# Deciding the top-k selection partly on GpSimd, cutting its ends into small steps, and splitting a third of the key blocks on GpSimd

## The chip, the cores and the metric

One NeuronCore of a Trainium2 chip runs the whole layer as one program. The metric is the device time of an execution in microseconds (us); the median of several executions counts. Engines: TensorE (PE), VectorE (DVE), ScalarE (ACT), GpSimd (POOL), and SyncE (SP), whose queue issues nearly all DMAs.

## What is computed

One layer of a streaming encoder on 2048 tokens of 1024 channels: a sparse attention with a learned index, a pooling mixer, gates, two layer norms and a gated feed-forward with a short convolution. What the change touches is the index and the attention:

```python
rel = relu(einsum('bqhd,bsd->bqhs', q_idx, k_idx) * idx_scale)        # 8 index heads
idx_score = einsum('bqh,bqhs->bqs', w_idx * head_w_scale, rel)        # one score per query and key
idx_score = where(admissible, idx_score, -inf)                        # chunk-causal
_, sel = top_k(idx_score, 256)                                        # each query keeps 256 keys
s = einsum('bqhd,bqkd->bqhk', q, k_lat[sel]) * attn_scale             # 8 heads, latent 128
p = softmax(where(valid, s, -inf)); out = einsum('bqhk,bqkd->bqhd', p, v_lat[sel])
```

## The kernel before

Matrix products in float32 are made of three passes: each operand is split into a rounded high part and a remainder, and `mm3` multiplies high by high, high by low and low by high. A split is two instructions (`split`, L394): normally a copy on ACT and a subtraction on DVE; with `pool=True` both on POOL.

The tokens are 16 blocks of 128, in 4 groups. The program runs the index projection of all groups, then for each group the pooling, query and gate projections (`run`, L2043), then attention (`attention`, L1377), the mixing and output projection, and the feed-forward. It is written out as one long list of instructions per engine, so each engine's order is fixed when the program is built.

**The selection as background work.** The reference's top-k and gather are replaced by a mask per block, added to the scores of all keys. `select` (L1069) finds each query's 256th largest index score by bisection on the bits of the float, 32 rounds. In each round every block's scores are counted against the trial value, part on DVE (`is_ge` with an accumulated sum), part on ACT (`Sign` with an accumulated sum). The blocks form two halves; `decide` (L1090) then makes the next trial value `F` of one half while the other half is counted: three small DVE instructions `g`, `h`, `F` on at most 4 columns. After the last round come the **ends**, block by block: a count of the strictly larger scores, a `Sign` on ACT, then on DVE a comparison, a running sum over the whole row (`tensor_tensor_scan`, L1162), two more comparisons and a subtraction, and the mask, which SP stores. There are three selections (`GROUPS`, L65): groups 0 and 1 together, group 2, group 3 (blocks 12 to 15).

These steps are generators. `turn` (L430), called after each small piece of the main work, decides at build time how many background steps go in: a credit grows by `RATE` (0.75) times the modelled PE time and each step costs its modelled DVE or ACT time; no step goes in while the modelled backlog of DVE or ACT behind PE is `SLACK` (3 us) or more. One `yield` of `select` ends a step.

**Attention.** A unit is one group of queries and one head, 32 in all, group after group. `scores` (L1229) makes scores and softmax weights of one block row after another; `values` (L1280) goes over the key blocks: four PE transposes into PSUM, a split of the result (ACT copy from PSUM, DVE subtraction from PSUM), and `LAG` = 3 key blocks later the product with the values. Once per unit POOL splits the next unit's queries (`split_q`, L1224). `load_mask` (L1192) fetches the mask of a block one block ahead of its use. If its selection has not ended, it runs the background work to the end on the spot:

```python
            while self.selected < b:
                if next(self.bg[0][1], "end") == "end":
                    self.bg.pop(0)
            self.settle()
            nc.sync.dma_start(m, self.d_msk[b])
```

All compute instructions are issued by one helper, so nearly all rows of the profile have its line, L133; tile names tell them apart: `m,cd<-b,F` a count on DVE, `g`, `h`, `F` the decision, `b<-p,b` the subtraction of a split from PSUM, `b<-m` and `b<-m,b` on POOL the split of the queries, `mx` (CUSTOM_DVE_ANT_0) the masked scores with their row minimum, `msk` a mask in memory, `vv` values, `q` queries.

## Time and profile before

| | |
|---|---|
| median of 3 runs (lowest, highest) | 3157.49 us (3157.08, 3163.70) |
| the profiled execution, its span | 3163.64 us, 3161.9 us |
| PE busy, mean granted clock | 3041.3 us (96%), 0.987 |
| DVE, ACT, POOL busy | 2433.5 (77%), 1605.4 (51%), 540.3 us (17%) |
| PE waits in the stretch 1308 to 1394 us: for DVE, three kinds | 24.3, 4.2, 2.7 us |

Times of instructions are in us from the span's start. Busy shares over the whole span mix stages with different limits; the rows further down are of single stretches. A busy PE is not always a PE at its peak, so the number of matmuls in a stretch is read beside its busy time.

### The profile page before, as it was taken

The numbers are of one execution on the slowest core, as the hardware profiler recorded it, in microseconds if no ns is written. First come the engines' busy times: TensorE is split into PE (matmuls) and PEld (weight loads), VectorE is DVE, ScalarE is ACT, GpSimd is POOL, SyncE is SP. The second block draws the span as 40 slices with busy tenths as digits, with TensorE's granted clock in tenths as the row PEclk, the third lists the DMA queues.
The fourth block names the chain that finished last, engine by engine and source line by source line (L and its number), as shares of the span: only waits on it lengthen the run. The fifth ranks groups of instructions, "written<-read, shape, count | busy, mean of one in ns | idle before, by whom it ended". The sixth has DMA issues, their size and how long they took to land. (4 is left out here: it accounts for less than half of the span.)

```text
span 3161.9 us, 43884 instructions
## 1 busy us (share of the span) xinstructions
PE 3041.3 (96%) x14750; PEld 2536.5 (80%) x14750; DVE 2433.5 (77%) x4552; ACT 1605.4 (51%) x3073; POOL 540.3 (17%) x528
## 2 busy tenths in 40 slices
PE   8999999999999999879999999999999999999998
PEld 8887778888888787768787778887778888888887
DVE  4578877896789899988775588998886655667776
ACT  3468846773578788657611144444442222433253
POOL 2002010010010221110231234554411111100011
PEclk9999999999999999989999999999999999999999
DMA  6758783765366332222264778887888866998753
GB/s 247 246 202 295 272 311 141 284 222 214 136 245 252 111 95 77 71 78 70 81 226 158 258 259 303 295 298 281 291 310 315 316 213 224 365 399 327 266 196 110
DMA packets 325872, 715.88 MB, mean 226 GB/s; under 512 B 27466, under 2 KB 132366, under 8 KB 325646
## 3 DMA queue, kind: packets, MB, share of 16 engines
q1 hardware_dynamic: 317006, 697.34, 62.0%
q10 hardware_dynamic: 8640, 15.73, 1.3%
q8 instruction: 117, 1.92, 0.3%
q14 instruction: 109, 0.89, 0.1%
HBM read 454.85 MB, written 258.11 MB: 225 GB/s over the span
## 5 line engine op out<-in xcount | busy, mean ns | idle before, releaser
L133 PE MATMUL p<-b,b 128*128 128x512 f32 (+3 forms) x12568 | 2828.8, 381 | 83.2 <-DVE mx L133 30.7
L133 PEld LDWEIGHTS p<-b,b 128*128 128x128 f32 x12568 | 2258.5, 190 | 524.6 <-DVE b L133 36.9
L133 DVE TENSOR_TENSOR b<-p,b 128x512 fp32r<-128x512 f32 (+3 forms) x626 | 395.4, 658 | 151.8 <-PE p L133 99.7
L133 ACT ACTIVATE b<-p 128x512 fp32r<-128x512 f32 (+11 forms) x638 | 363.2, 606 | 278.9 <-PE p L133 265.9
L133 ACT ACTIVATE b<-b 128x512 fp32r<-128x512 f32 (+3 forms) x344 | 270.8, 805 | 322.5 <-DVE b L133 138.5
L133 DVE TENSOR_TENSOR b<-b,b 128x1024 fp32r<-128x1024 f32 (+6 forms) x302 | 338.9, 1133 | 84.3 <-ACT b L133 37.1
L133 ACT ACTIVATE m<-b,F 128x448 bf16<-128x448 f32 (+3 forms) x448 | 366.1, 820 | 47.9 <-DVE F L133 34.3
L133 DVE TENSOR_SCALAR_CACHE_REDUCE m<-b,F 128x512 bf16<-128x512 f32 (+6 forms) x476 | 372.5, 808 | 8.3 <-DMA gm<-m 4.3
L133 ACT ACTIVATE b<-m 128x512 fp32r<-128x512 f32 x215 | 133.2, 627 | 332.4 <-DVE m L133 119.9
L133 DVE SCALAR_TENSOR_TENSOR b<-b,cw,b 128x1023 f32<-128x1023 f32 (+1 forms) x176 | 246.3, 1411 | 69.7 <-ACT b L133 68.7
L133 ACT ACTIVATE b<-b,cw 128x1024 f32<-128x1024 f32 x88 | 106.9, 1236 | 270.8 <-DVE b L133 270.8
L133 POOL TENSOR_TENSOR b<-b,b 128x1024 f32<-128x1024 f32 (+3 forms) x62 | 148.6, 2401 | 491.0 <-DVE b L133 283.2
L133 PE MATMUL p<-ident,b 128*128 128x128 f32 x1248 | 198.1, 278 | 17.4 <-DVE b L133 7.0
L133 ACT ACTIVATE b<-b,mx 128x1024 f32<-128x1024 f32 (+2 forms) x192 | 171.5, 895 | 81.0 <-DVE mx L133 79.0
L133 DVE TENSOR_TENSOR b<-m,b 128x512 fp32r<-128x512 f32 x215 | 153.8, 723 | 55.0 <-ACT b L133 52.9
L133 PEld LDWEIGHTS p<-ident,b 128*128 128x128 f32 x1248 | 154.0, 142 | 52.5 <-DVE b L133 11.4
L133 DVE SCALAR_TENSOR_TENSOR b<-b,ws,b 128x768 f32<-128x768 f32 (+5 forms) x154 | 153.4, 1023 | 55.5 <-ACT b L133 53.0
L133 DVE CUSTOM_DVE_ANT_0 b<-p,b 128x1024 f32<-128x1024 f32 (+7 forms) x128 | 125.6, 984 | 35.0 <-PE p L133 27.2
L133 PE MATMUL p<-kst,b 128*128 128x384 f32 (+3 forms) x656 | 149.0, 360 | 2.8 <-ACT b L133 2.0
L133 ACT ACTIVATE m<-p 128x512 f32<-128x512 f32 (+2 forms) x172 | 100.7, 585 | 79.1 <-PE p L133 75.6
L133 PEld LDWEIGHTS p<-kst,b 128*128 128x128 f32 x656 | 111.7, 189 | 24.1 <-ACT b L133 13.6
L133 DVE TENSOR_TENSOR b<-p,m 128x512 f32<-128x512 f32 x132 | 89.8, 682 | 10.7 <-PE p L133 10.6
(125 smaller groups left out, 1496.7 us busy)
## 6 DMA issues: line engine op xcount, KB each, us to landing
b<-wk SPq DMA_DIRECT2D x339, 512.0 KB
wk<-b SPq DMA_DIRECT2D x211, 512.0 KB
b<-h SPq DMA_DIRECT2D x88, 512.0 KB
b<-in_w_ffn_up_dram SPq DMA_DIRECT2D x44, 512.0 KB
h<-b SPq DMA_DIRECT2D x44, 512.0 KB
b<-vv SPq DMA_DIRECT2D x80, 256.0 KB
hs<-b SPq DMA_DIRECT2D x33, 512.0 KB
b<-hs SPq DMA_DIRECT2D x33, 512.0 KB
```

What stands on the lines that cost most here:

```text
L133: return f(*args, **kw)
```

## The change

- `decide`: `g` and `h` are made by three POOL instructions, issued together behind the first count of the other half; only `F` stays on DVE.
- `RATE` 0.80 instead of 0.75; the model's cost of the running sum is doubled (`SCAN`); while a selection's end runs, a background step may go in up to a backlog of 4 us.
- The ends yield after nearly every instruction, and the running sum is cut into pieces of 512 columns, each started from the last column of the one before.
- `load_mask` also fetches the block after next, if its selection has ended.
- While background work is left and from group 1 on, every third key block's split in `values` goes another way: ACT copies PSUM to a tile, POOL makes both parts from it.

```diff
-SLACK = 3.0
+SLACK, END_SLACK = 3.0, 4.0
+PIECE = 512
-RATE = 0.75
+RATE = 0.8
-SCAN = 1.04
+SCAN = 2.12
...
-        while self.bg and self.clocks.backlog() < SLACK and self.credit > 0:
+        while self.bg and self.clocks.backlog() < (END_SLACK if self.ending else SLACK) and self.credit > 0:
...
             step = next(gen, "end")
+            self.ending = step == END
...
-            nc.vector.scalar_tensor_tensor(g_, cd, 2.0, ca, op0=OP.mult, op1=OP.subtract)
+            nc.gpsimd.tensor_scalar(g_, cd, 2.0, -lim, op0=OP.mult, op1=OP.add)
+            nc.gpsimd.tensor_tensor(g_, g_, ca, op=OP.subtract)
+            nc.gpsimd.tensor_scalar(h, g_, 0.0, float(2 ** bit) if bit < 31 else -1.0, op0=OP.is_lt, op1=OP.mult)
             yield
...
-                nc.vector.tensor_scalar(h, g_, lim, float(2 ** bit), op0=OP.is_lt, op1=OP.mult)
-                yield
                 nc.vector.scalar_tensor_tensor(f2, h, 2 ** (bit - 1) if bit else 0, F[k],
...
-                    if pend:
+                    if pend and i == 0:
                         next(pend, None)
...
-                nc.vector.tensor_tensor_scan(cu, eq, eq, 0.0, op0=OP.add, op1=OP.max)
+                yield END
+                for c0 in range(0, N, PIECE):
+                    e = slice(c0, min(c0 + PIECE, N))
+                    nc.vector.tensor_tensor_scan(cu[:, e], eq[:, e], eq[:, e], cu[:, c0 - 1:c0] if c0 else 0.0,
+                                                 op0=OP.add, op1=OP.max)
+                    yield END
...
-        if b >= NB or b in self.masks:
+        if b >= NB or b in self.masks or not wait and b > self.selected:
             return
...
                 self.load_mask(b + 1)
+            if h == 0 and rb < RB - 2 or h == H - 1 and rb >= RB - 2:
+                self.load_mask(b + 2, False)
...
-            self.split(pt[:, 0, c:], pt[:, 1, c:], ps.rearrange("p h q -> p (h q)")[:, c:])
+            src = ps.rearrange("p h q -> p (h q)")[:, c:]
+            if self.bg and g and kb % 3 == 1:
+                whole = self.T([P, 512])[:, c:]
+                nc.scalar.activation(whole, src, AF.Copy)
+                self.split(pt[:, 0, c:], pt[:, 1, c:], whole, pool=True)
+            else:
+                self.split(pt[:, 0, c:], pt[:, 1, c:], src)
```

As built, DVE issues 47 subtractions and 384 decision instructions fewer and 24 pieces of running sums more. POOL issues 576 decision instructions and 47 pairs of split instructions more. PE's 14750 matmuls are the same; from the one that ran at 1394 us on they stand in the same order.

**SP's queue where attention passes to group 3** (`vv` values, `q` queries, `msk_175` to `msk_178` the masks of blocks 12 to 15; L461 is `settle`). Before:

```order
574 L1213 DMA m_15969<-q_158 128x1x512
575 L461 DMA at_181<-m_15906 128x512
576 L461 DMA msk_175<-b_15913 128x1664
577 L1206 DMA b_15910<-msk_175 128x1664
582 L461 DMA msk_176<-b_15991 128x1792
583 L1206 DMA b_15978<-msk_176 128x1792
585 L461 DMA msk_177<-b_16077 128x1920
586 L1206 DMA b_16040<-msk_177 128x1920
587 L461 DMA msk_178<-b_16151 128x2048
588 L1206 DMA b_16138<-msk_178 128x2048
```

Now (L440 is `turn`):

```order
564 L440 DMA msk_177<-b_15615 128x1920
568 L1221 DMA m_15911<-q_157 128x1x512
569 L440 DMA at_181<-m_15852 128x512
573 L1221 DMA m_16133<-q_158 128x1x512
574 L440 DMA msk_178<-b_16098 128x2048
578 L1214 DMA b_16235<-msk_175 128x1664
579 L1214 DMA b_16296<-msk_176 128x1792
580 L1221 DMA m_16350<-q_158 128x1x512
586 L1214 DMA b_16359<-msk_177 128x1920
587 L1214 DMA b_16406<-msk_178 128x2048
```

Before, each of the four masks was stored by `settle` right ahead of its load. Now all four are stored by `turn` before the first is loaded (the stores of blocks 12 and 13 are rows 531 and 548).

**DVE at the running sum of block 14** (`SCALAR_TENSOR_TENSOR` with one input is a running sum; `p` is PSUM). Before:

```order
2315 L133 TENSOR_TENSOR b_16035<-p_4869_16033,b_16035 128x128
2316 L133 TENSOR_SCALAR b_16066<-b_16065 128x1920
2317 L133 SCALAR_TENSOR_TENSOR b_16067<-b_16066 128x1920
2318 L133 TENSOR_TENSOR m_16132<-p_4827_15872,m_16133 64x512
2319 L133 SCALAR_TENSOR_TENSOR nd_16072<-b_16067,fx_16051,cg_16050 128x1
2321 L133 TENSOR_SCALAR b_16066<-b_16067,nd_16072 128x1920
2322 L133 TENSOR_TENSOR b_16065<-b_16065,b_16066 128x1920
2323 L133 TENSOR_SCALAR b_16077<-b_16065 128x1920
```

Now:

```order
1746 L135 TENSOR_SCALAR b_15166<-b_15165 128x1920
1747 L135 TENSOR_TENSOR b_15196<-p_4622_15191,b_15196 128x512
1748 L135 ISA b_15217,mx_15180<-p_4627_15213,b_14619,mx_15180 128x512
1750 L135 SCALAR_TENSOR_TENSOR b_15167<-b_15166 128x512
1751 L135 TENSOR_TENSOR b_15227<-p_4629_15222,b_15227 128x512
1752 L135 SCALAR_TENSOR_TENSOR b_15167<-b_15166,b_15167 128x512
1753 L135 ISA b_15251,mx_15243<-p_4637_15244,b_14495 128x1024
1761 L135 SCALAR_TENSOR_TENSOR b_15167<-b_15166,b_15167 128x512
1764 L135 SCALAR_TENSOR_TENSOR b_15167<-b_15166,b_15167 128x384
```

The end that stood as one run of long instructions now stands as pieces between attention's own instructions.

**POOL across one unit of group 1.** Before (`b<-m` the queries' split, COPY part of a head's result):

```order
163 L133 TENSOR_SCALAR b_13977<-m_13896 128x512
164 L133 TENSOR_TENSOR b_13977<-m_13896,b_13977 128x512
165 L133 COPY m_14013<-rinv_13756 128x4x64
166 L133 COPY m_14013<-rinv_13894 128x4x64
167 L133 TENSOR_SCALAR b_14118<-m_14051 128x512
```

Now (`b<-b` a key block's split):

```order
790 L135 TENSOR_TENSOR b_14690<-b_14691,b_14690 128x512
791 L135 COPY m_14717<-rinv_14427 128x4x64
793 L135 TENSOR_SCALAR b_14755<-b_14756 128x512
794 L135 TENSOR_TENSOR b_14755<-b_14756,b_14755 128x512
795 L135 TENSOR_SCALAR b_14811<-b_14812 128x128
797 L135 TENSOR_SCALAR b_14845<-b_14846 128x512
798 L135 TENSOR_SCALAR b_14873<-m_14765 128x512
799 L135 TENSOR_TENSOR b_14845<-b_14846,b_14845 128x512
800 L135 TENSOR_TENSOR b_14873<-m_14765,b_14873 128x512
```

Three or four key blocks' splits have come into each unit, and in row 798 the queries' split stands between the two instructions of one of them.

## Rows read from the trace of the kernel before

**Rows 1.** The page: the span, PE's and DVE's line (busy us, share, instructions) and PE's line of the 40 slices (tenths).

```profile
span 3161.9 us, 43884 instructions
...
PE 3041.3 (96%) x14750; PEld 2536.5 (80%) x14750; DVE 2433.5 (77%) x4552; ACT 1605.4 (51%) x3073; POOL 540.3 (17%) x528
...
PE   8999999999999999879999999999999999999998
```

**Rows 2.** Busy time by stretch: from and to in us, length, then busy us (instructions) of PE, PEld, DVE, ACT and POOL, granted PE clock, DMA share, GB/s.

```profile
300.00:420.00 120.00, 109.50 (x479) 87.42 (x478) 105.54 (x408) 105.81 (x289) 0.10 (x1) 0.97 0.83 293
480.00:1040.00 560.00, 560.00 (x2565) 465.43 (x2564) 467.80 (x1066) 383.18 (x686) 35.86 (x50) 1.00 0.57 208
880.00:1040.00 160.00, 160.00 (x712) 132.54 (x711) 147.09 (x369) 126.03 (x229) 16.30 (x22) 1.00 0.60 224
1114.00:1308.00 194.00, 188.02 (x1122) 158.04 (x1121) 182.95 (x409) 158.94 (x336) 29.92 (x40) 1.00 0.26 78
1308.00:1394.00 86.00, 54.86 (x258) 44.59 (x258) 71.61 (x120) 39.62 (x75) 14.43 (x8) 0.80 0.26 90
1394.00:1560.00 166.00, 164.28 (x979) 139.42 (x977) 134.23 (x246) 120.74 (x233) 18.94 (x22) 1.00 0.21 66
```

**Rows 3.** What PE waited for from 1308 to 1394 us: us in total, times, longest us.

```profile
PE p L133 <- DVE mx L133: 24.3, 4, 7.9
PE p L133 <- DVE m L133: 4.2, 1, 4.2
PE p L133 <- DVE b L133: 2.7, 1, 2.7
```

**Rows 4.** The timeline around 1356 us: start, us, engine, instruction, and in brackets the idle time before and what ended it.

```profile
1355.93 4.45 DVE L133 TENSOR_TENSOR_SCAN b<-b 128x1920 f16<-128x1920 f16 x1
...
1356.46 4.98 POOL L133 TENSOR_TENSOR b<-m,b 128x512 fp32r<-128x512 f32 x1
...
1361.01 1.11 PE L133 MATMUL p<-ident,b 128*128 128x128 f32 x4 [4.20 <-DVE m L133]
```

**Rows 5.** DVE's instructions by shape from 1308 to 1394 us: count | busy us, mean ns of one | idle before.

```profile
L133 DVE TENSOR_TENSOR_SCAN b<-b 128x2048 f16<-128x2048 f16 x1 | 4.4, 4426 | 0.0
...
L133 DVE TENSOR_TENSOR_SCAN b<-b 128x1664 f16<-128x1664 f16 x1 | 3.6, 3624 | 0.0
...
L133 DVE TENSOR_TENSOR b<-p,b 128x128 fp32r<-128x128 f32 x3 | 0.8, 282 | 0.0
```

**Rows 6.** DVE's instructions by shape over the whole span, same columns.

```profile
L133 DVE SCALAR_TENSOR_TENSOR g<-cd,ca 128x2 f32<-128x2 f32 x160 | 28.5, 178 | 7.8 <-ACT m L133 3.7 <-DVE m L133 0.5
L133 DVE TENSOR_SCALAR h<-g 128x2 int32<-128x2 f32 x160 | 28.1, 176 | 4.5
...
L133 DVE TENSOR_TENSOR_SCAN b<-b 128x512 f16<-128x512 f16 x1 | 1.2, 1233 | 0.0
```

**Rows 7.** DVE's instructions by shape from 1114 to 1394 us: the splits from PSUM, the counts (in the decisions and at the ends together), and the decision's last instruction. Columns as in Rows 5.

```profile
L133 DVE TENSOR_TENSOR b<-p,b 128x512 fp32r<-128x512 f32 x110 | 72.4, 685 | 9.2 <-ACT b L133 8.6
...
L133 DVE TENSOR_SCALAR_CACHE_REDUCE m<-b,F 128x896 bf16<-128x896 f32 x12 | 13.6, 1137 | 0.0
...
L133 DVE TENSOR_SCALAR_CACHE_REDUCE m<-b,F 128x1024 bf16<-128x1024 f32 x8 | 10.0, 1273 | 0.0
...
L133 DVE TENSOR_TENSOR b<-p,b 128x256 fp32r<-128x256 f32 x16 | 6.6, 412 | 0.0
...
L133 DVE TENSOR_SCALAR_CACHE_REDUCE m<-b,F 128x768 bf16<-128x768 f32 x5 | 5.0, 1006 | 0.0
...
L133 DVE SCALAR_TENSOR_TENSOR F<-h,F 128x2 int32<-128x2 int32 x9 | 1.6, 175 | 0.2
```

**Rows 8.** POOL's splits of the queries from 1114 to 1308 us, by shape, columns as in Rows 5.

```profile
L133 POOL TENSOR_TENSOR b<-m,b 128x512 fp32r<-128x512 f32 x13 | 16.8, 1292 | 1.1
L133 POOL TENSOR_SCALAR b<-m 128x512 fp32r<-128x512 f32 x13 | 8.1, 620 | 149.0 <-PE p L133 67.3 <-ACT b L133 32.3 <-DMA m<-q 27.1
```

**Rows 9.** POOL's timeline at a layer norm, small instructions of one column.

```profile
1627.48 1.31 POOL L133 TENSOR_SCALAR lv<-mv 128x1 f32<-128x1 f32 x1 [2.25 <-DVE mv L133]
...
1629.53 0.20 POOL L133 TENSOR_TENSOR lt<-lr 128x1 f32<-128x1 f32 x1
1629.80 0.19 POOL L133 TENSOR_TENSOR lt<-lt,lv 128x1 f32<-128x1 f32 x1
1630.08 0.19 POOL L133 TENSOR_SCALAR lt<-lt 128x1 f32<-128x1 f32 x1
```

**Rows 10.** DVE's timeline at the same place.

```profile
1627.43 1.28 DVE L133 SCALAR_TENSOR_TENSOR b<-b,mv,b 128x1024 f32<-128x1024 f32 x1
```

**Rows 11.** PE's timeline in a unit of group 2: the transposes of its first five key blocks are the x4 rows with ident; the product of the second key block begins at 1264.20.

```profile
1259.86 0.60 PE L133 MATMUL p<-ident,b 128*128 128x128 f32 x4
...
1264.20 1.07 PE L133 MATMUL p<-b,b 128*128 128x512 f32 x4
```

**Rows 12.** ACT's timeline there: the copies of the first three key blocks.

```profile
1260.66 1.55 ACT L133 ACTIVATE b<-p 128x512 fp32r<-128x512 f32 x3
```

**Rows 13.** DVE's timeline there: the subtractions of the first two.

```profile
1261.28 1.28 DVE L133 TENSOR_TENSOR b<-p,b 128x512 fp32r<-128x512 f32 x2
```

**Rows 14.** The timeline of POOL and DVE together at 1312 us.

```profile
1312.42 3.62 DVE L133 TENSOR_TENSOR_SCAN b<-b 128x1664 f16<-128x1664 f16 x1
1312.42 4.03 POOL L133 TENSOR_SCALAR b<-m 128x512 fp32r<-128x512 f32 x1 [15.54 <-PE p L133]
```

More of the change, by code (lines that the diff above doesn't have):

```diff
@@ L70 @@
 PAUSE = "pause"
+END = "part of a selection's end"
 GRAIN = 1
-RATE = 0.75
+RATE = 0.8
 CAP = 1.5
@@ L362, in __init__ @@
         self.credit = self.seen = 0.0
+        self.ending = False
     def _name(self, s):
@@ L1096, in decide @@
             lim = 2.0 * TOPK - 1.0 - ws[k]
-            nc.vector.scalar_tensor_tensor(g_, cd, 2.0, ca, op0=OP.mult, op1=OP.subtract)
+            nc.gpsimd.tensor_scalar(g_, cd, 2.0, -lim, op0=OP.mult, op1=OP.add)
+            nc.gpsimd.tensor_tensor(g_, g_, ca, op=OP.subtract)
+            nc.gpsimd.tensor_scalar(h, g_, 0.0, float(2 ** bit) if bit < 31 else -1.0, op0=OP.is_lt, op1=OP.mult)
             yield
             if bit == 31:
-                nc.vector.tensor_scalar(h, g_, lim, -1.0, op0=OP.is_lt, op1=OP.mult)
-                yield
                 nc.vector.tensor_scalar(f2, h, 0x40000000, None, op0=OP.bitwise_xor)
             else:
-                nc.vector.tensor_scalar(h, g_, lim, float(2 ** bit), op0=OP.is_lt, op1=OP.mult)
-                yield
                 nc.vector.scalar_tensor_tensor(f2, h, 2 ** (bit - 1) if bit else 0, F[k],
@@ L1142, in select @@
                                             accum_out=c[:, j * nh + i:j * nh + i + 1])
-                yield
+                    yield END
             cg, fx, ab = (self.sml([P, 4], tag=x)[:, :nh] for x in ("cg", "fx", "ab"))
@@ L1159, in select @@
                 nc.scalar.activation(sg[:, N - w:], back[b], AF.Sign, bias=tn[:, i:i + 1])
-                yield
+                yield END
                 nc.vector.tensor_scalar(eq, sg, 0.0, None, op0=OP.is_equal)
-                nc.vector.tensor_tensor_scan(cu, eq, eq, 0.0, op0=OP.add, op1=OP.max)
+                yield END
+                for c0 in range(0, N, PIECE):
+                    e = slice(c0, min(c0 + PIECE, N))
+                    nc.vector.tensor_tensor_scan(cu[:, e], eq[:, e], eq[:, e], cu[:, c0 - 1:c0] if c0 else 0.0,
+                                                 op0=OP.add, op1=OP.max)
+                    yield END
                 nd = self.sml([P, 1], tag="nd")
@@ L1166, in select @@
                 nc.vector.tensor_scalar(nd, nd, float(TOPK), None, op0=OP.add)
-                yield
                 nc.vector.tensor_scalar(eq, cu, nd, None, op0=OP.is_gt)
+                yield END
                 nc.vector.tensor_tensor(sg, sg, eq, op=OP.subtract)
+                yield END
                 m = self.T([P, N], BF16)
@@ L1174, in select @@
                 self.selected = max(self.selected, b)
-                yield
+                yield END
     def attn_load(self):
@@ L1190, in attn_setup, with load_mask @@
         self.masks, self.vv = {}, {}
-    def load_mask(self, b):
+    def load_mask(self, b, wait=True):
         nc = self.nc
-        if b >= NB or b in self.masks:
+        if b >= NB or b in self.masks or not wait and b > self.selected:
             return
```

## The prediction, made before the result

> **What bounds the kernel now.** I read the page first: PE is busy 96% of the span, and its slices are full but for a dip in the 17th and 18th of 40, around 1300 to 1400 us [rows 1]. So this kernel can only be helped where PE is not full, and the next view is busy time by stretch [rows 2]. From 480 to 1040 us, projections with two selections behind them, PE is busy every microsecond. There nothing can be gained, only lost. From 1114 to 1308 us, attention on groups 1 and 2 with the last selection beside it, PE idles 194 - 188.0 = 6.0 us and DVE is 94% busy. From 1308 to 1394 us PE does 258 matmuls in 86 us, at a granted clock of 0.80. From 1394 us, attention with no selection left, PE does 979 in 166 us, 5.90 per us, with DVE at 81%. At that rate the 258 would take 43.7 us. The stretch loses **42.3 us**, by far the largest loss in the program, and in it PE waits for DVE alone [rows 3].
>
> Why DVE: this is where `load_mask` of block 12 finds the selection unended and runs the rest at once. The four running sums of blocks 12 to 15 stand here, 3.6 to 4.4 us each [rows 5]. The timeline shows one of them: it starts at 1355.93, attention's next DVE instruction and PE stand behind it, and PE is idle 4.20 us; POOL's split of the queries takes 4.98 us beside it [rows 4]. PE's low clock follows from the gaps, and is part of the 42.3 us.
>
> **The change part by part.** Durations come from the profiled execution, 3163.64 us for a span of 3161.9. It is as slow as the slowest of the three timed runs and 6.2 us over their median; no row says where those 6 us lie, so I subtract the same gain from the median.
>
> *The forced end goes.* In the order as built, the last decision's count stands ahead of the matmul that ran at 1111 us before (it stood at 1267), and the four masks are stored ahead of those that ran at 1166, 1206, 1267 and 1308. The first of the loads follows the last store, so `load_mask` finds all four selected. What is late next is DVE's ordinary backlog, in the row from 1394 on 1.7 us of PE in 166. I take the whole **-42.3 us**. In the bounds, a quarter may come back as waits around the change of group: -32 to -42.3.
>
> *Does DVE have room for the ends between 1114 and 1308?* From 1114 to 1394 DVE is busy 183.0 + 71.6 = 254.6 us [rows 2]. Of the 25 counts there, 8 belong to the ends (one of 768 columns, four of 896, three of 1024: 9.4 us). The other 17 are 28.6 - 9.4 = 19.2 us and move ahead, and so do nine decisions of about 0.52 us, 4.7 us [rows 6, 7]. The 47 subtractions that go to POOL are 34 of 512 columns at 0.685, 5 of 256 at 0.412 and 8 of 128 at 0.282: 27.6 us [rows 5, 7]. The pieces add starts: by the sums of 2048 and 1664 columns one column takes 2.09 ns, so a piece of 512 at 1.233 us has a start of 0.16; twelve more of them are 2.0 us [rows 5, 6]. That leaves 205 us of DVE for 194 + 43.7 = 238 us, 86%. PE's idle share was 1.0% with DVE at 81% and 3.1% with DVE at 94% [rows 2]; at 86% I read 1.9%, 4.5 us against the 6.0 + 0.4 that are counted so far. **-2 us**, bounds -6 and +4.
>
> *POOL's key blocks.* A pair of 512 columns takes 0.62 + 1.29 us [rows 8] where DVE took 0.685, so POOL gets about 72 us more in the 194 (34 pairs of 1.91 and 13 shorter). The question is how late a block comes. In the unit at 1259 us the second key block's transposes start at 1259.86 and its product starts at 1264.20 [rows 11]. Its ACT copy is the second of three in 1.55 us and ends at about 1261.7 [rows 12]; DVE's subtraction, the second of two, ends at 1262.56 [rows 13], 1.6 us in hand. POOL would start at 1261.7, and with its 1.91 us and two hand-overs of about 0.1 end at 1263.8, 0.4 us in hand. Where the queries' split stands between the two instructions, as the order shows it about once per unit, its 0.62 us turn that into 0.2 us late. So most blocks just make it. For the 14 units I take 0.35 us each, **+5 us**. The bounds are 0 and all 47 blocks late by 0.6 us, +28.
>
> *Decisions on POOL.* Small POOL instructions follow each other every 0.27 us [rows 9], so three take 0.8 us and with the hand-overs about 1 us, against 0.35 us for `g` and `h` on DVE [rows 6]. In the last group this lies beside two counts of the other half, 2.1 us [rows 7]; only in the first selection are the smaller half's counts about as short as the decision. There each decision gives DVE back 0.35 us and may make it wait as long. PE idles 10.5 of 120 us there, from 300 to 420 us [rows 2]: **0**, bounds -5 and +5.
>
> *More background earlier.* 17 counts come into the stretch before 1045 us. DVE is busy 147.1 of 160 us from 880 to 1040 with PE full [rows 2]. The counts add 19.2 us, and some 60 decisions without `g` and `h` take away 60 x 0.354 = 21 us. ACT gets about as many microseconds more as DVE for its counts, from 126 of 160 us to at most 145. **0**; the upper bound is +5, since the row from 300 to 420 us shows a PE that idles where DVE and ACT are both at 88%. The masks' earlier load changes SP's order by a few rows; no wait of the sum hangs on it, and I cost it at nothing: its cover is that SP's next transfers are wanted a unit later.
>
> Sum: -42.3 - 2 + 5 = **-39.3 us**, 3124.3 for an execution like the profiled one, and 3157.5 - 39.3 = 3118 us for the median.
>
> **The rivals.**
>
> *POOL and DVE block each other* (chance 0.18). At 1312 us POOL's split, 0.62 us elsewhere, took 4.03 us, and it began with the 3.62 us of a running sum [rows 14, 8]. A small POOL instruction took 1.31 us beside a DVE instruction of two SBUF tiles, where others take 0.19 [rows 9, 10]. So POOL stands still while DVE runs such instructions, and the pieces of 1.23 us now stand between POOL's new pairs. The ends have 32 larger instructions on SBUF alone; if each waits half of POOL's 1.29 us, DVE gets 21 us more, 226 of 238 us or 95%, where PE's idle share is about 3.3%, 7.9 us: instead of -2 that is +1.5. If in turn half of the 47 pairs lose half a piece beyond what they have in hand, 24 x 0.6 = 14 us of PE go. Together -42.3 + 1.5 + 5 + 14 = -22: 3135 us, and 3128 to 3147 for stronger and weaker collisions. Against it: the subtractions from PSUM that fill most of DVE's time show the same 0.685 us everywhere.
> The Trainium skill speaks against this change here: SBUF — State Buffer, Who interferes with whom, has the two engines share a port pair that one holds for a whole instruction, DVE when it reads two SBUF tiles or runs a two-port mode, while "the other **fully blocks**"; Perfetto Trace Analysis, Optimizing Scalar/DVE Operations, adds that moving work between the two "might not help". By that rule the trace agrees in rows 14 and 10, and the time would be this rival's.
>
> *Slower: POOL's queue becomes attention's bound* (chance 0.05). One place: the product of a key block that POOL splits. With 47 of them, every 0.1 us of mean lateness costs 4.7 us; the gain of 44 us is gone at 0.94 us and the time is 0.2% up, 3164 us, at 1.08 us. That needs POOL to end about 1.5 us later than my unit shows, as when each pair stands behind a whole split of the queries (1.91 us) or two pieces. At 1.3 us of lateness it is 3174 us. For it: PE's queue is in order, and POOL would be busy (29.9 + 72) / 194 = 53% of the stretch. Against it: only one block in three goes this way, and the queries' split stands in front of it once per unit.
>
> *More than forecast* (0.07): the first selection's stretch also gets back half of its 10.5 us, and POOL's blocks are all in time: -42.3 - 2 - 5 - 4 = -53, 3104 us.
>
> *The change does not do what it says* (0.02): the end is still forced. The order speaks against it, and it would leave 3157 us.
>
> **How the numbers follow.** The forecast, 3108 to 3128 us, gets 0.66; the collision 0.18; more than forecast 0.07; slower 0.05; 0.02 for the end that stays and 0.02 for POOL's lateness between, 3147 to 3164. About 0.2% (6 us) is what a measurement of this kernel can tell from no change: faster 0.91, same 0.04, slower 0.05. The range leaves out the slower cases and half of the top of the collision: 3104 to 3142 us.
>
> **What would show it.** In the profile after: no stretch in attention with PE below 90% and a clock of 1.00 throughout, running sums of 1.2 us between attention's instructions, and no wait of PE for `mx` over 3 us. DVE between the same matmuls as 1114 and 1394 busy near 205 us. PE's waits for POOL's `b` a few us in all; if they are over 15 us, the POOL term failed. POOL's pairs near 0.62 and 1.29 us; if their means are 1 us longer, the collision is at work. The stretch to 1040 us as long as before within 5 us; if it is longer, the decisions' or the share's term failed. A time over 3142 us or a PE stall like that at 1356 us would make the prediction wrong.

## The result: half a per cent faster, less than half of the gain that was forecast

| | median us | against before, 95% interval |
|---|---|---|
| before, same chip (5 runs) | 3157.49 | |
| the change (5 runs) | 3141.71 | 0.9946, 0.9935 to 0.9957 |
| forecast | 3118 | 0.9875 |

The change gains 15.8 us where 39.3 were forecast. The profiled execution took 3146.39 us, span 3144.6. Lines of its page (busy time, then busy tenths in 40 slices), to be read against [rows 1]:

```profile
PE 3041.0 (97%) x14750; PEld 2529.1 (80%) x14750; DVE 2369.5 (75%) x4145; ACT 1609.3 (51%) x3073; POOL 743.1 (24%) x1198
...
PE   8999899999999989999999999999999999999998
...
POOL 2004220230032355500231234554411111100011
PEclk9999999999999999999999999999999999999999
```

The dip around 1300 to 1400 us is gone, but slices 5 and 15, full before, now have an 8. What they lost shows when both programs are cut at the same matmuls, counted from the program's start, and the lengths compared. The windows of the program before (window; its length; then busy us and instructions of PE, PEld, DVE, ACT, POOL; clock; DMA):

```profile
277.50:426.50 149.00, 137.81 (x602) 110.24 (x601) 131.72 (x510) 126.03 (x343) 3.10 (x9) 0.98 0.85 299
1040.00:1061.50 21.50, 20.80 (x102) 17.28 (x100) 18.25 (x55) 16.45 (x37) 5.26 (x6) 1.00 0.47 132
1113.80:1182.10 68.30, 67.55 (x418) 57.82 (x416) 64.33 (x139) 58.25 (x118) 13.77 (x18) 1.00 0.32 96
1182.10:1307.00 124.90, 119.67 (x703) 99.61 (x702) 117.89 (x269) 99.89 (x218) 16.15 (x22) 1.00 0.22 68
1307.00:1393.50 86.50, 55.36 (x262) 44.99 (x262) 72.55 (x121) 40.12 (x77) 14.43 (x8) 0.80 0.27 90
```

and of the change, between the same matmuls:

```profile
276.10:437.30 161.20, 140.78 (x601) 110.01 (x600) 122.91 (x423) 125.80 (x341) 40.38 (x156) 0.97 0.79 274
1050.70:1077.60 26.90, 23.17 (x102) 18.43 (x100) 22.16 (x57) 20.10 (x43) 10.40 (x30) 0.94 0.40 118
1128.70:1206.90 78.20, 70.12 (x418) 57.62 (x416) 68.34 (x127) 55.90 (x110) 46.81 (x58) 1.00 0.33 96
1206.90:1331.60 124.70, 119.64 (x702) 99.81 (x701) 113.50 (x232) 94.30 (x201) 63.65 (x76) 1.00 0.24 73
1331.60:1377.00 45.40, 44.74 (x261) 37.76 (x260) 37.23 (x75) 32.50 (x67) 8.66 (x10) 1.00 0.44 141
```

The last row is the forced end: 86.5 us have become 45.4, **-41.1**, at a clock of 1.00 in place of 0.80. Three rows pay for it: the **first selection** (matmuls 1700 to 2300), +12.2 us; the **start of attention** (5100 to 5200), +5.4; **group 1** of attention (5486 to 5900), +9.9. Group 2 (5900 to 6600) is as long as before, -0.2. That makes -13.8. Up to the start of the last matmul the traces differ by -17.6; the 3.8 us between are found behind attention (3.9 us from 1709 to 1947 us), where every kernel below is 2 to 7 us shorter than the profiled execution of before as well, whatever its edit: that execution seems to have been slow there.

In the first selection DVE now waits for POOL. What DVE and PE waited for there in all (us, times, longest), before:

```profile
DVE g L133 <- ACT m L133: 2.0, 4, 1.2
...
PE p L133 <- ACT b L133: 5.6, 5, 3.2
PE p L133 <- DVE b L133: 5.5, 5, 2.2
```

after:

```profile
DVE F L135 <- POOL h L135: 31.5, 42, 2.6
...
PE p L135 <- ACT b L135: 12.9, 10, 2.7
PE p L135 <- DVE b L135: 7.4, 8, 2.1
```

A plain case of such a decision, from the timeline of the change (start, us, engine, instruction):

```profile
309.42 0.81 DVE L135 TENSOR_SCALAR_CACHE_REDUCE m<-b,F 128x576 bf16<-128x576 f32 x1
310.15 0.08 DVE L135 DVE_READ_ACCUMULATOR m<-b,F 128x1 f32 x1
...
310.31 0.19 POOL L135 TENSOR_SCALAR g<-cd 128x4 f32<-128x4 f32 x1 [3.54 <-DVE m L135]
310.59 0.20 POOL L135 TENSOR_TENSOR g<-g,ca 128x4 f32<-128x4 f32 x1
...
310.88 0.23 POOL L135 TENSOR_SCALAR h<-g 128x4 int32<-128x4 f32 x1
...
311.14 0.16 DVE L135 SCALAR_TENSOR_TENSOR F<-h,F 128x4 int32<-128x4 int32 x1 [0.91 <-POOL h L135]
```

The chain takes the 1 us that was forecast for it, but as built `F` stands directly behind its own half's last count: DVE is idle 0.91 us. The two counts of the other half, which were to cover it, come after `F`. Of the first selection's 64 decisions, 15 have no such count in front of `F` in the order as built, 40 have one, and 9 have two or three.

### The profile page after: what moved, and what is told of

The parts are those of the page before. It is cut to its first block, busy times and chain, and to the rows that moved or that the text cites. A ratio compares the mean times of both kernels' runs of the same rounds, so it can differ in the third digit from the quotient of the medians.

```text
span 3144.6 us, 44249 instructions
## 1 busy us (share of the span) xinstructions
PE 3041.0 (97%) x14750; PEld 2529.1 (80%) x14750; DVE 2369.5 (75%) x4145; ACT 1609.3 (51%) x3073; POOL 743.1 (24%) x1198
## 5 line engine op out<-in xcount | busy, mean ns | idle before, releaser
L135 DVE TENSOR_TENSOR b<-p,b 128x512 f32<-128x512 f32 (+5 forms) x579 | 371.2, 664 | 153.5 <-PE p L135 97.3
L135 POOL TENSOR_TENSOR b<-b,b 128x512 fp32r<-128x512 f32 (+4 forms) x109 | 202.2, 1856 | 492.2 <-DVE b L135 300.0
L135 POOL TENSOR_SCALAR g<-cd 128x2 f32<-128x2 f32 x192 | 45.2, 235 | 759.3 <-DVE m L135 692.0
L135 PEld LDWEIGHTS p<-kst,b 128*128 128x128 f32 x656 | 111.4, 189 | 27.3 <-ACT b L135 15.4
```

The lines of the kernel that those rows point to most:

```text
L135: return f(*args, **kw)
```

## The experiments

Sixteen kernels, in four batches, each beside the kernel before on the same chip. All cuts are made as above; a step is the length between two matmuls, less that of the program before. "Lag" is worked out from each trace: the start of a DVE instruction, less the start of the matmul behind which it stands in the program, as a mean over matmuls 5100 to 5150. Other ways to take this mean move it by about half a microsecond in most kernels, but to 0.9 in x13 and to 4.0 in x16, where few DVE instructions stand there. The runs are from three chips, so kernels are compared by their ratios to the kernel before.

| kernel | median us | ratio, interval | first sel. | lag | attention start | group 1 | group 2 | end |
|---|---|---|---|---|---|---|---|---|
| before | | | 0 | 0.4 | 0 | 0 | 0 | 0 |
| the change | 3141.71 | 0.9946, 0.9935–0.9957 | +12.2 | 4.4 | +5.4 | +9.9 | -0.2 | -41.1 |
| x1 | 3137.86 | 0.9937, 0.9922–0.9951 | +7.8 | 4.2 | +3.9 | +9.8 | -0.3 | -41.0 |
| x2 | 3138.48 | 0.9937, 0.9922–0.9951 | +6.7 | 5.7 | +5.5 | +6.8 | +3.8 | -40.9 |
| x3 | 3198.69 | 1.0128, 1.0111–1.0144 | +23.1 | 10.6 | +12.8 | +11.3 | -0.3 | -41.0 |
| x4 | 3142.40 | 0.9949, 0.9934–0.9964 | +6.0 | 4.2 | +3.9 | +4.2 | +7.1 | -36.2 |
| x5 | 3137.64 | 0.9930, 0.9915–0.9945 | 0.0 | 6.9 | +6.7 | +11.7 | +3.3 | -39.7 |
| x6 | 3143.92 | 0.9948, 0.9931–0.9964 | +7.0 | 7.0 | +7.2 | +12.6 | +3.5 | -39.8 |
| x7 | 3142.36 | 0.9945, 0.9930–0.9960 | 0.0 | 11.8 | +19.1 | +0.8 | +3.1 | -42.0 |
| x8 | 3144.85 | 0.9950, 0.9935–0.9965 | +0.1 | 9.8 | +13.8 | +6.1 | -3.3 | -41.9 |
| x9 | 3133.65 | 0.9921, 0.9897–0.9945 | +6.2 | 4.6 | +5.0 | +9.5 | +0.7 | -41.1 |
| x10 | 3134.48 | 0.9915, 0.9897–0.9932 | +0.5 | 5.5 | +11.8 | +4.5 | +2.3 | -41.8 |
| x11 | 3154.18 | 0.9981, 0.9970–0.9992 | +6.1 | 8.2 | +12.1 | +3.3 | +2.0 | -36.3 |
| x12 | 3148.14 | 0.9967, 0.9954–0.9979 | +1.8 | 0.4 | 0.0 | +10.1 | +15.7 | -36.4 |
| x13 | 3131.35 | 0.9916, 0.9902–0.9931 | +6.4 | 1.9 | -0.1 | +7.0 | 0.0 | -39.3 |
| x14 | 3144.90 | 0.9957, 0.9942–0.9973 | +7.8 | 4.3 | +3.7 | +7.7 | +6.5 | -41.1 |
| x15 | 3144.69 | 0.9963, 0.9950–0.9977 | +6.4 | 4.4 | +4.6 | +13.6 | +7.5 | -41.9 |
| x16 | 3137.58 | 0.9940, 0.9921–0.9960 | +0.5 | 7.5 | +6.5 | +8.3 | +2.7 | -40.0 |

Kernels with the same first selection (x1, x4, x9, x13, x14, x15) give steps of 6.0 to 7.8 there, and x12, whose first selection is that of the kernel before, gives +1.8: a step is known to one or two microseconds. The table leaves out the other stretches; most of the rest is between matmuls 0 and 1700 (-6.1 to +3.4) and 5200 and 5486 (-2.8 to +5.6).

### The first selection: decisions or share?

**x1**, `g` and `h` of the first selection on DVE:

```diff
+        on_pool = halves[0][0] >= 2 * RB
...
+            if on_pool:
+                nc.gpsimd.tensor_scalar(g_, cd, 2.0, -lim, op0=OP.mult, op1=OP.add)
...
+            else:
+                nc.vector.scalar_tensor_tensor(g_, cd, 2.0, ca, op0=OP.mult, op1=OP.subtract)
...
-                    if pend and i == 0:
+                    if pend and (i == 0 or not on_pool):
```

> The change, but with g and h of the first selection (groups 0 and 1) back on DVE; every other instruction stands at the same matmul as in the changed kernel. Theory A (decisions): DVE's F there waits for POOL's chain with one count or less in between, and PE loses 12 us from this between its matmuls 1700 and 2300 (277 to 427 us before); so that step against before falls from +12 us to between -1 and +2, and the time from 3141.7 to about 3130 us. Rival B (share): the background's share of 0.80 packs DVE and ACT more densely, and that costs the 12 us; the step stays at +12 or rises, since DVE gets 64 x 0.35 = 22 us more: 3142 to 3150 us.

The step fell to +7.8, between the two theories.

**x2**, all decisions on DVE (the change's lines of `decide` and of the count loop undone):

```diff
-                    if pend and i == 0:
+                    if pend:
```

> The change, but with all decisions back on DVE. Theory A: the first selection's step is gone as in the run before, and if the 5.4 us that PE lost where attention begins (matmuls 5100 to 5200) come from decisions too, they go as well: about 3125 us, 3130 if they do not. The last mask is stored just ahead of its load, so the forced end does not return under either theory. Rival B: 3142 to 3150 us.

The time is between those of the two theories. The first selection agrees with x1, and attention's start keeps its +5.5: decisions are not what is late there. The later selections behind the projections are as long with decisions on DVE as on POOL.

**x3**, two more instructions in the chain:

```diff
             nc.gpsimd.tensor_tensor(g_, g_, ca, op=OP.subtract)
+            nc.gpsimd.tensor_scalar(g_, g_, 1.0, 1.0, op0=OP.mult, op1=OP.mult)
+            nc.gpsimd.tensor_scalar(g_, g_, 1.0, 1.0, op0=OP.mult, op1=OP.mult)
```

> The change with two more small POOL instructions in each decision that leave the value as it is, 2 x 0.27 = 0.54 us more per decision; nothing else moves. Theory A: in the first selection DVE waited 37 us for POOL in 53 waits and PE lost 12 us, a third; 64 decisions x 0.54 = 35 us of later F give about +12 us (6 to 30) in that step, nothing in the later selections where PE was full, 1 to 3 us where attention begins: about 3155 us. Rival B: the decisions are not what PE waits for, no more than +2 us: 3142 to 3144 us.

57 us more than the change, far over either theory. The first selection pays 11 of them. Most of the rest is where I expected nothing: +17.6 in the second selection (matmuls 3200 to 3500) and +11.1 in the third (4900 to 5100), behind projections that had kept PE full, and 7.4 more at attention's start. What DVE waited for in this kernel from 300 to 1100 us:

```profile
DVE F L135 <- POOL h L135: 122.2, 146, 3.2
```

So the decisions' price of nothing in the later selections stands on a margin of less than the 0.54 us that were added to each.

**x5**, x1 at the old share while the first selection runs; **x6**, the change with that alone:

```diff
-RATE = 0.8
+RATE = {3: 0.75, 2: 0.8, 1: 0.8, 0: 0.8}
...
-        self.credit = min(self.credit + RATE * (pe - self.seen), CAP)
+        self.credit = min(self.credit + RATE[len(self.bg)] * (pe - self.seen), CAP)
```

> The kernel with the first selection's g and h on DVE, and the share back at 0.75 while the first selection runs (0.80 after it). What was measured: PE's step between matmuls 1700 and 2300 is +12.2 us for the change, +7.8 with g and h on DVE. Theory AB (both): the decisions cost 4.5 us of it and the share the other 7 to 8; so the step is now 0 (-1 to +2), and the time about 7 us below that kernel's 3137.9, 3131 us. Rival P (something else that moved to POOL or the placement of the first selection costs it): the step stays near +7, 3138 us.

> As the run before, but with the first selection's g and h on POOL: the change with the share at 0.75 while the first selection runs, and nothing else. Theory AB, added: the step is +5 us, the decisions alone, and the time 3136 us. If the two only cost together (a decision that is late hurts where DVE and ACT are packed), the step is 0 to +2 and the time 3131 us, as the run before. If the decisions cost it all whatever the share, +10 to +12 and 3141 us.

The steps 0.0 (x5), +7.0 (x6), +7.8 (x1) and +12.2 (the change) are a square: decisions on POOL cost 4 to 7 us, the share of 0.80 costs 5 to 8. Both times came out 6 to 8 us over what theory AB expected; 3 of them are the chip, on which the kernel before took 3161.3 us (3158.0 where x1 ran). This stretch of x5 and of x6, columns as above:

```profile
276.80:425.70 148.90, 137.72 (x601) 110.28 (x600) 131.64 (x510) 126.12 (x343) 3.11 (x9) 0.98 0.84 299
```

```profile
273.50:429.50 156.00, 139.90 (x602) 110.71 (x601) 121.98 (x417) 128.09 (x348) 41.50 (x163) 0.97 0.82 290
```

In x6 DVE has 10 us less to do and PE takes 7 us longer: what DVE saves it spends waiting. x5 gains little if anything in total over x1 (0.9930 against 0.9937), since 2.8 us more are lost at attention's start and 5.5 in groups 1 and 2, into which background was put off.

### What buys the end, and what it costs elsewhere

**x11**, the kernel before with a share of 0.80 alone:

```diff
-RATE = 0.75
+RATE = 0.8
```

> The kernel before with the share at 0.80 and nothing else. As built, the last mask is then stored 33 matmuls ahead of its load, so the end is no longer forced. Theory S (the share alone buys the end, and costs the first selection 8 us and attention's start 4): steps +8, +4, and -41 between 6600 and 6860, with a few us of waits for the whole running sums of 3.6 to 4.4 us in group 2: 3133 us. Rival W (whole sums and the subtractions that POOL does not take leave PE waiting): steps of 10 to 25 us between 5486 and 6600 more than in the change: 3140 to 3155 us.

**x12**, the kernel before with POOL's key blocks alone:

```diff
-            self.split(pt[:, 0, c:], pt[:, 1, c:], ps.rearrange("p h q -> p (h q)")[:, c:])
+            src = ps.rearrange("p h q -> p (h q)")[:, c:]
+            if self.bg and g and kb % 3 == 1:
+                whole = self.T([P, 512])[:, c:]
+                nc.scalar.activation(whole, src, AF.Copy)
+                self.split(pt[:, 0, c:], pt[:, 1, c:], whole, pool=True)
+            else:
+                self.split(pt[:, 0, c:], pt[:, 1, c:], src)
```

> The kernel before with POOL's key blocks (one in three, from group 1 on, while the background runs) and nothing else; share 0.75, decisions on DVE, ends in whole steps. As built the last mask is stored 20 matmuls ahead of its load. Theory K: first selection and attention's start 0, group 1 +6 to +10 from late blocks, the end -41: 3126 us. Rival W (whole running sums in attention stall PE up to 3 us each, eight in all behind group 1 and 2, and delay POOL's pairs): 10 to 20 us more, 3136 to 3146 us.

Each alone ends the forced end (-36.3, -36.4), and each gives most of it back elsewhere: x11 in the first selection, at attention's start (+12.1) and behind it (+5.6 between matmuls 5200 and 5486), x12 in groups 1 and 2 (+25.8). x11 is as slow as rival W had it, but not where W had it: groups 1 and 2 cost 5.3 us. Its +12.1 is not the share's price by itself, since x2 has the same share, also with all decisions on DVE, and pays 5.5. In x11 the last selection's last decision stands at matmul 5112 (5593 in x2), and the first whole running sum, 3.61 us at 1074.86, already stands among attention's first scores, where PE waits 3.0 us for `mx`. PE's waits in group 2 of x12:

```profile
PE p L133 <- POOL b L133: 6.4, 3, 2.8
PE p L133 <- DVE b L133: 3.6, 3, 3.0
PE p L133 <- DVE mx L133: 2.6, 6, 0.6
```

That fits rival W, whole running sums in attention, and the time lies 2 us over its range. **x15** is x1 with each end in whole steps; as the ends' other `yield END` are taken out or made plain `yield` too, the backlog of 4 us that the change allows in an end goes with them:

```diff
-                for c0 in range(0, N, PIECE):
-                    e = slice(c0, min(c0 + PIECE, N))
-                    nc.vector.tensor_tensor_scan(cu[:, e], eq[:, e], eq[:, e], cu[:, c0 - 1:c0] if c0 else 0.0,
-                                                 op0=OP.add, op1=OP.max)
-                    yield END
+                nc.vector.tensor_tensor_scan(cu, eq, eq, 0.0, op0=OP.add, op1=OP.max)
```

> The kernel with the first selection's g and h on DVE, but each end in whole steps as before the change; the model's cost of a running sum, the share and the last decision's place stay. Theory E (small steps matter in attention): running sums of 3.6 to 4.4 us and the comparisons behind them stand in one piece between attention's DVE instructions, PE stalls up to 2 us for each of eight such pieces, and POOL's pairs come later: 5 to 16 us more between 5486 and 6600, 3143 to 3154 us. Rival F (the steps only cost starts, 2 us in all): 0 to 2 us less, 3136 to 3138 us.

Groups 1 and 2 cost 21.1 us in place of 9.5: the small steps, with that backlog, are worth 11.6 us, at an unchanged place of the last decision. In group 2, PE waits longest for a block of POOL and one of DVE, over 3 us each:

```profile
PE p L135 <- POOL b L135: 3.9, 2, 3.2
PE p L135 <- DVE b L135: 3.5, 2, 3.3
```

The Trainium skill has this as a rule (Perfetto Trace Analysis, Optimizing Scalar/DVE Operations): where engines that are not saturated cause gaps on others, breaking up their instructions may let work finish sooner. x15 agrees: 11.6 us for ends in small steps with pieces of 512 columns.

No run takes out the doubled modelled cost of a running sum, the backlog of 4 us, or the masks' earlier load by itself; what each is worth is not shown.

### The start of attention

**x9**, x1 with the first unit's queries loaded and split earlier:

```diff
                 self.attention_start()
+                self.load_mask(0)
+                self.load_unit(0)
...
+                if j == 3 and g + 1 == NG and i == 0:
+                    self.split_q(0)
```

> The kernel with the first selection's g and h on DVE, and besides the first unit's queries loaded and split half a projection step earlier; nothing else moves. PE lost 3.9 us there where attention begins (matmuls 5100 to 5200; 5.4 in the change), waiting 1.7 us for this split and 1.9 us for scores. Theory Q: the load stands on SP behind a store that waits for DVE, and for a tile that a count on ACT still holds, so the background's backlog is in front of attention's first operand; loaded earlier, the step falls to 0 to +1 and the time by 3 to 4 us to 3134. Rival: PE then waits for the scores' row minimum on DVE instead, as the backlog is still there; step +3 to +4, 3138 us.

The step stayed, +5.0: the rival held. PE waits 0.3 us for the split now, but longer for DVE's row minimum:

```profile
PE p L135 <- DVE mx L135: 5.1, 2, 2.8
```

(The 4 us of lower time lie in other stretches, the interval is wide, and I don't count them.) What goes with the step is the lag: 0.4 us and 0 in the program before and in x12, 4.2 to 4.6 us and +3.7 to +5.4 in six kernels, 8 to 12 us and +12 to +19 in x11, x8, x3 and x7; x10, 5.5 us and +11.8, fits it least; x2, x5, x6 and x16 lie between, 5.7 to 7.5 us and +5.5 to +7.2. In the change, PE's longest gap there is at attention's first matmuls:

```profile
1063.76 1.92 PE L135 MATMUL p<-b,b 128*128 128x128 f32 x9 [2.02 <-ACT b L135]
```

**x13** takes the lag away:

```diff
+            if j == 3 and g + 1 == NG:
+                self.hold = True
...
-        while self.bg and self.clocks.backlog() <
+        while self.bg and not self.hold and self.clocks.backlog() <
...
     def attention(self):
+        self.hold = False
```

> The kernel with the first selection's g and h on DVE, and no background step between the set-up of attention and its beginning, the last 24 us of the projections. In the kernels so far, DVE's instructions between matmuls 5000 and 5100 started 0.0 us behind PE's place in the program before, 5.2 to 5.4 us behind it in the change, 8.9 and 7.4 in kernels that lost 6.7 and 12.1 us there. Theory L (lag): projections keep PE full and hide how late DVE and ACT run; attention's first scores need them, and the lag is paid there. With the pause the lag is 0 to 1 us and the step from 5100 to 5200 falls from +3.9 to 0 to +1; the background that is moved, some 18 us, comes into group 1 and 2 and costs 0 to 4 us: 3134 to 3138 us. Rival: the step comes from attention's own loads and stays +3 to +5: 3138 to 3142 us.

The lag falls to 1.9 us and the step to -0.1. The time, 3131.35 us, is the lowest of all kernels; by its ratio, 0.9916, it can't be told from x10's 0.9915. The stretch in x13, and the same gap:

```profile
1044.20:1065.60 21.40, 20.83 (x101) 17.26 (x100) 11.82 (x34) 10.63 (x25) 6.91 (x17) 1.00 0.49 151
...
1055.26 0.97 PE L135 MATMUL p<-b,b 128*128 128x128 f32 x5 [0.29 <-DVE b L135]
```

DVE is busy 11.8 us where it was 22.2 in the change. The pause takes out the backlog and also the counts that stood between attention's first DVE instructions; which of the two costs how much, the run does not part.

### Group 1

**x4**, x1 with POOL's key blocks from group 2 on:

```diff
-            if self.bg and g and kb % 3 == 1:
+            if self.bg and g > 1 and kb % 3 == 1:
```

> The first of these kernels (first selection's g and h on DVE), but POOL splits key blocks only from group 2 on, not in group 1. Theory K (key blocks late): PE lost 10 us between matmuls 5486 and 5900, all group 1, because POOL's blocks come late; that step falls to about +3, and the time to 6 us below that kernel's. Rival D (the ends' small steps between attention's DVE instructions cost it): DVE gets some 13 subtractions back, 9 us, and the step stays at +10 or rises; the time is 0 to 5 us above that kernel's. In both the last mask is stored some 16 matmuls ahead of its load, which may cost a wait of up to 3 us.

Group 1 falls from +9.8 to +4.2 as theory K has it, but the ends come later, and group 2 and the end give back 12 us. As some of the ends leave group 1 too, 5.6 us is the most that POOL's key blocks can be said to cost there. **x14**, x1 with one key block more between transposes and product:

```diff
-LAG = 3
+LAG = 4
```

> The kernel with the first selection's g and h on DVE, and the product with the values four key blocks behind the transposes in place of three. Theory K (POOL's blocks are late by up to 0.9 us, mostly where a pair stands behind the queries' split): no PE wait for POOL is left in attention, and the step from 5486 to 5900 falls from +9.8 to about +4, the time by 6 us to 3132. Rival D (DVE, filled by the ends, is what PE waits for): the step stays at +8 to +11 and the time at 3138 us.

K fell in part: PE's waits for POOL in group 1 shrink from 3.8 us in six to 0.4 in one, and the step only from +9.8 to +7.7; group 2 loses 6.8 us, waiting for DVE. The time, 3144.9 us, is over both theories. Why DVE is later there was not settled. PE's waits in group 1, of the change

```profile
PE p L135 <- POOL b L135: 3.8, 6, 0.9
PE p L135 <- DVE b L135: 3.0, 4, 1.3
```

and of x14:

```profile
PE p L135 <- DVE b L135: 4.2, 5, 1.9
PE p L135 <- DVE nd L135: 1.5, 1, 1.5
PE p L135 <- POOL b L135: 0.4, 1, 0.4
```

One late block of the change, on POOL's timeline:

```profile
1151.72 0.53 POOL L135 TENSOR_SCALAR b<-b 128x128 fp32r<-128x128 f32 x1 [4.45 <-ACT b L135]
1152.22 0.61 POOL L135 TENSOR_SCALAR b<-m 128x512 fp32r<-128x512 f32 x1
1152.81 0.45 POOL L135 TENSOR_TENSOR b<-b,b 128x128 fp32r<-128x128 f32 x1
1153.22 1.28 POOL L135 TENSOR_TENSOR b<-m,b 128x512 fp32r<-128x512 f32 x1
1154.47 1.52 POOL L135 TENSOR_SCALAR b<-b 128x512 fp32r<-128x512 f32 x1
1156.08 1.27 POOL L135 TENSOR_TENSOR b<-b,b 128x512 fp32r<-128x512 f32 x1
```

on DVE's:

```profile
1153.63 1.96 DVE L135 TENSOR_TENSOR_SCAN b<-b 128x512 f16<-128x512 f16 x1
```

and on PE's:

```profile
1156.05 0.50 PE L135 MATMUL p<-b,b 128*128 128x512 f32 x1 [0.30 <-POOL b L135]
1157.41 0.73 PE L135 MATMUL p<-b,b 128*128 128x512 f32 x2 [0.85 <-POOL b L135]
```

The pair waits behind the whole split of the queries (`b<-m`), and then its first instruction takes 1.52 us in place of 0.62, beside a piece of a running sum. That piece itself takes 1.96 in place of 1.23: it begins at 1153.63, while POOL's `b<-m,b` runs until 1154.50. Such long ones are few. From group 1 to where the last mask is loaded, 1128.7 to 1377 us, the pairs of 512 columns took (count | busy us, mean ns):

```profile
L135 POOL TENSOR_TENSOR b<-b,b 128x512 fp32r<-128x512 f32 x34 | 44.2, 1300 | 2.5
L135 POOL TENSOR_SCALAR b<-b 128x512 fp32r<-128x512 f32 x34 | 22.9, 674 | 51.6 <-ACT b L135 51.5
```

### Versions that might beat both

**x7**: x1 with shares 0.75, 0.85, 0.85 and key blocks from group 2 on. **x8**: the same with 0.90. **x10**: x9 with shares 0.75, 0.82, 0.82. **x16**: x13 with 0.75, 0.82, 0.83. Of x16:

```diff
+RATE = {3: 0.75, 2: 0.82, 1: 0.83, 0: 0.8}
```

> A version that might beat both: first selection's g and h on DVE at a share of 0.75, a share of 0.85 in the other two selections, and POOL's key blocks from group 2 on only. The last selection's decisions then end where attention begins, and its last mask is stored 185 matmuls ahead of its load. Theory K (POOL's key blocks cost group 1 some 5 to 6 us; without them the later ends cost 7 us in group 2): the step 1700 to 2300 is 0, the one from 5486 to 5900 +4, the one from 5900 to 6600 0 to +2; if the projections still cover 0.85: 3125 us. Rival C (0.85 is more than the projections cover: DVE was busy 147 of 160 us there before): PE loses 5 to 15 us between matmuls 2500 and 5100: 3130 to 3140 us.

> As the run before with a share of 0.90 in the later two selections: half of the last selection's ends then lie ahead of attention. If the projections cover it, group 1's step falls to +1 and the time to 3121 us; by rival C the step between 2500 and 5100 is +10 to +30 us and the time 3130 to 3150 us.

> A version that might beat both: the early queries, the first selection on DVE at a share of 0.75, and 0.82 after it; key blocks and small ends as in the change. If the terms add: step 1700 to 2300 0, attention's start +1, group 1 (5486 to 5900) +5 to +10, the end gone, -41: about 3123 us. If 0.82 is too much behind the projections or at attention's start, 3128 to 3138 us.

> A version that might beat both: first selection on DVE at a share of 0.75, then 0.82 and, in the last selection, 0.83; the pause ahead of attention; key blocks and small ends as in the change. If the terms add: step 1700 to 2300 0, attention's start 0 to +1, groups 1 and 2 +10 to +16, end -40: 3157.5 - 26 = 3131 us, or 3127 if groups 1 and 2 cost no more than in the change. If the background that is moved into attention costs what the pause saves: 3134 to 3138 us.

In none do the terms add up, but x10 is clear of the change (0.9915 against 0.9946, and the intervals do not meet). A denser background behind the projections saves groups 1 and 2 (x7: +3.9 in all) and is paid at attention's start (+19.1); in x8 the projections no longer cover it either, as rival C had it: +12.0 us between matmuls 2500 and 5100. In x16 the pause did not suffice for the denser background: DVE ran 9.1 us behind just ahead of it (matmuls 5090 to 5100; 4.7 in x13), and the step is +6.5. A longer pause was not run.

## Why the prediction was wrong

The two terms put at 0, decisions on POOL and more background earlier, are the steps that failed. In their place the trace shows +12.2 us in the first selection and +5.4 at attention's start. The prediction had named a sign for this: the stretch that ended at 1040 us was to stay as long within 5 us, and the same matmuls now end at 1050.7.

- **The forced end goes, -42.3: right.** -41.1, and -36 to -42 in all sixteen kernels. The share or the key blocks alone move the end far enough.
- **Decisions on POOL, 0: wrong; this step failed.** The chain's 1 us was right. Its cover was not: I put two counts of the other half beside it, from the code, where the order as built has one or none between a half's counts and its `F` (55 of the first selection's 64). Measured +4 to +7 us in the first selection, inside or just over the bound of 5. The 0 for the later selections held (x2), on a margin that x3 found.
- **More background earlier, 0 to +5: wrong, too small; this step failed too.** The share costs 5 to 8 us in the first selection, where PE's waits for ACT go from 5.6 us to 11.3 (x1), and 5.4 at the start of attention. The row I had named against it, 300 to 420 us [rows 2], was the one that paid. The 480 to 1040 us that were to hide the counts did hide them; the lag they left behind, for which the prediction had no term, was paid at the next stage's first operand.
- **POOL's key blocks and DVE's room, +5 and -2: mis-sized.** Together +9.7 us (group 1 and 2) where +3 was forecast. Key blocks are at most some 5.6 of it (x4 against x1); 3.8 us are waits for POOL itself, and the queries' split in front of a pair is the cause that the prediction had named. DVE between 1114 and 1394 us was busy 219.1 us where I had 205. Of these 14 us, 5 are the pieces of the running sums (23.3 us for a forecast 18.3). Most of the others are a slip of the sum: it took the instructions' own durations off a busy time in which neighbours overlap (in the rows at 309 us, by 0.08 us). The durations fell by 44.0 us and the busy time by 35.7.
- **POOL and DVE block each other, 14 us: a part is there.** The rows around 1154 us show it both ways, but the mean of POOL's pairs in attention is 0.67 and 1.30 us, near the 0.62 and 1.29 of [rows 8]. That the time came out in this rival's upper half, and 0.3 us inside the range, is luck: 17.6 of the 27.3 us that were lost lie ahead of the stretch that this rival is about. The Trainium skill's rule on the shared port (SBUF — State Buffer, Who interferes with whom) has one engine wait for the whole instruction of the other; the trace agrees for that pair, which ends its first instruction 0.4 us after the running sum.
- **POOL's queue as the bound:** no. PE's waits for POOL are 5.8 us in the whole run.
- **More than forecast:** no. The -4 us in its sum has no row behind it; POOL's blocks all in time would be 0.

Corrected sum for the traces: -41.1 (end) + 12.2 (first selection: decisions and share) + 5.4 (lag at attention's start) + 9.7 (groups 1 and 2) = -13.8, and some 4 us that the profiled execution of before seems to have lost behind attention.

## What to carry to other kernels

Where a stage keeps its bounding engine full, look at how late the others run behind it, not only at whether they fit: the lag is free until the next stage's first operand, and in x13 a pause of the background just ahead of that point cost less than the lag. Read the cover of a moved step in the order as built, between its input and its first user, never in the source. And when two parts of a change each suffice for the gain, price each part's cost by itself: here x13, with decisions off POOL in the first selection and a pause ahead of attention, gains 25 us.

## What was not expected of the hardware

Two small POOL instructions more per decision, 0.54 us, cost 57 us of a kernel whose PE had seemed full: the length of a chain that crosses engines in every round counts 192 times, wherever its cover is thin. A running sum's piece of 512 columns took 1.44 to 1.80 us in the mean beside POOL's new pairs (13 pieces from 1128 to 1378 us) and 1.23 in the program before [rows 6]. The difference comes with the pairs. Pieces in group 1 of x1:

```profile
L135 DVE TENSOR_TENSOR_SCAN b<-b,b 128x512 f16<-128x512 f16 x4 | 5.9, 1478 | 0.0
L135 DVE TENSOR_TENSOR_SCAN b<-b 128x512 f16<-128x512 f16 x2 | 4.2, 2114 | 0.0
```

and of x4, where POOL has no pairs in group 1:

```profile
L135 DVE TENSOR_TENSOR_SCAN b<-b,b 128x512 f16<-128x512 f16 x2 | 2.6, 1277 | 0.0
L135 DVE TENSOR_TENSOR_SCAN b<-b 128x512 f16<-128x512 f16 x1 | 1.2, 1212 | 0.0
```

In the trace of the change the one that begins later is the one that waits. The six of the 13 pieces that took 1.50 us or more all began while a POOL instruction with two inputs had 0.4 to 1.2 us left to run; the other seven took 1.22 to 1.30 us, and where POOL began an instruction beside one of them, that instruction ended after the piece.
